# A decoder block's schedule: convolution steps metered by what VectorE already holds, small work moved between engines, a second pair of buffers for the second half's x

## The chip, the core and the metric

The kernel runs on one core of a Trainium2 chip. Its engines work side by side, each through its own list of instructions in order: TensorE (PE in the profile) multiplies matrices into PSUM, VectorE (DVE) and ScalarE (ACT) do elementwise work, GpSimd (POOL) elementwise work on SBUF, and SyncE (SP) issues most transfers. The metric is the device time of one execution in microseconds (us), as a median over runs.

## The reference

One layer of a decoder block over 2048 tokens of width 1024, in float32:

```python
h = rms_norm(x, norm_w) * (1 + scale) + shift            # scale, shift, gate = silu(c) @ w_ada + b_ada
a, b, g_conv, q, k, v, g_attn, m_conv, m_attn = split(h @ w_in)
u = a * sigmoid(b);  u = depthwise_causal_conv(u, 31 taps) + bias
u = silu(layer_norm(u)) * silu(g_conv);  y_conv = u @ w_conv_out
q, k = rope(rms_norm(q)), rope(rms_norm(k))              # 12 heads of 128
# three head groups, windows (128, 512, 2048) read with stride (1, 4, 16);
# their outputs are mixed by a softmax over the groups' log denominators
y_attn = (o * silu(g_attn)) @ w_attn_out
out = x + gate * ((sigmoid(m_conv) * y_conv + sigmoid(m_attn) * y_attn) @ w_out)
```

## The kernel before

**Products and slots.** Nearly all of PE's time goes to `h @ w_in`. Float32 operands are split into a high and a low part (`h`, `l`, names ending in _hi and _lo, and sh, sl for weights), and a product of two is three matmuls: high by high, low by high, high by low. A *quad* is a pair of 128-column blocks over half the tokens, computed with seven block products instead of eight; each product is twelve matmuls of 128x512 (L326) and is called a *slot*. There are 562 slots, in two halves of 1024 tokens: in each, first Q, K and V quads (half 0: slots 16 to 127; half 1: 282 to 407), then the quads of the gates, of the convolution's input (`ab_quad`) and of attention's gate (`ag_quad`), up to slots 281 and 561. Afterwards come the convolution branch's layer norm and the two branch projections (`ya`, `yc`, L1587), then the output projection (L1869).

**What goes on beside.** For each product ACT rounds the weights to the high part (L263) and POOL or DVE subtracts for the low part (L264; `lo_engines` names the products of a quad whose split goes to DVE). POOL also forms the weight differences of the seven-product scheme (L258). DVE adds the products' PSUM banks (L349, L364, L526).

Each of twelve *rotations* per half takes two heads of Q or K: ACT squares, DVE joins the squares (L609), PE sums them over the head (L618, pss), ACT adds the epsilon, PE turns the sums round (L629), POOL raises them to the power -1/2 (L638, `roots`), while DVE does the rotary products (L688 to L695). For K the factor must go back to rows: ACT `upper` (L650), DVE `lower` (L654), PE `turned_back` (L658, pwk), DVE `widen` (L662, rwk), PE `spread` (L667, rsk), DVE `key_scale` (L672). Group 2 is the one with stride 16; its rotations start a little later within their quad.

Each *ab quad* gives some 50 convolution steps to DVE (`conv_parts`): even taps and odd taps separately (L383 to L399), a join, and mixed taps on the sum of both (L415), which give the odd output tokens; POOL forms the sum. Attention runs in *units*, one begun every second slot: scores on PE, mask and minimum on DVE (L820), exponentials on ACT, transposes on PE (L836) copied by DVE into `pT` (L838), values on PE (L861), the mix of groups on DVE (L853, L864), a transpose back (L882). The second half's x is normalised beside the first half's slots 21 and later, four rounds of four tiles (`later_load`, `later_scale`, `later_sum`, lines 1319 to 1340), with one buffer a tile; attention starts when this is done, at slot 80.

**What sets the order.** The program walks through the slots and calls, at fixed places in each, what was booked with `at_slot(s, f, where)`: the places are, in order, enter, load, act, pe, vec, prepare, act2, then the product (with mid after its sixth matmul), tail and store. An engine's instructions stand in the order in which they were emitted, except in the gates of each half, where a scheduler orders DVE, ACT, POOL and SP; PE's list is always as emitted. Convolution steps are given out by count at the end of a slot:

```python
due += CONV_RATE                 # 3.1
if not conv_todo:
    due = 0.0
count = int(due)
due -= count
run_conv(count)
```

## Time and profile before

| | before |
|---|---|
| median of 3 runs | 2426.02 us (2423.64 to 2428.11) |
| profiled execution, its own time | 2425.99 us |
| span of the profile | 2423.9 us |
| PE, DVE, ACT, POOL busy | 2302.4, 1820.0, 1074.2, 1090.0 us |
| instructions | 34180 |

Busy time of an engine is the time in which at least one of its instructions runs. A row of the waits says which engine waited at which tile and line, for whose result, and then the total, the number of times and the longest in us. A timeline row has the start, the duration, the engine, the line and operation, and in brackets the idle time before it with what ended it. A row of windows has the window, its length, then PE, PEld (weight loads), DVE, ACT and POOL busy with the number of instructions, the clock granted to PE as a share, the busy share of the transfer engines and the GB/s moved.

### The profile page before, as it was taken

The page shows a single profiled execution, that of the slowest core. Times are in us where ns is not written, and L with a number is a line of the kernel's source. Part 1 is how long each engine was busy: PE and PEld are TensorE (multiplying, and loading weights), DVE is VectorE, ACT ScalarE, POOL GpSimd, SP SyncE. Part 2 cuts the span into 40 slices and gives each one's busy share as a digit, 9 for nine tenths or more (in the row PEclk, how much of TensorE's full clock was granted, in tenths as well). Part 3 has the DMA queues.
Part 4 walks back from the last instruction along what each step waited for, and adds up shares of the span by engine and source line. Part 5 has one row for each costly group of instructions (what it writes and reads, how often), then busy time and mean ns, then how long its engine had stood idle before and what let it go on. Part 6 is the DMA issues. An engine that isn't in the chain of part 4 may idle for free.

```text
span 2423.9 us, 34180 instructions
## 1 busy us (share of the span) xinstructions
PE 2302.4 (95%) x11242; PEld 1874.7 (77%) x11242; DVE 1820.0 (75%) x2976; ACT 1074.2 (44%) x2187; POOL 1090.0 (45%) x844
## 2 busy tenths in 40 slices
PE   6998889999989999899999999999999999999999
PEld 4776668778777888787778887887888877888887
DVE  6788786563999999937766557459999987787644
ACT  4753345445553444554445444553444444332221
POOL 2466454456445779855423333345556640000221
PEclk9998999999999999999999999999999999999999
DMA  7655655667554445643556665755444469876553
GB/s 254 197 175 187 200 182 168 195 187 244 177 178 141 166 165 187 230 153 107 169 173 182 200 185 161 251 170 187 142 132 154 141 211 333 291 237 192 179 160 105
DMA packets 304104, 451.50 MB, mean 186 GB/s; under 512 B 29236, under 2 KB 132788, under 8 KB 303928
## 3 DMA queue, kind: packets, MB, share of 16 engines
q1 hardware_dynamic: 289656, 423.62, 55.1%
q10 hardware_dynamic: 14272, 25.72, 2.9%
q8 instruction: 88, 1.44, 0.2%
q14 instruction: 88, 0.72, 0.1%
HBM read 284.98 MB, written 164.24 MB: 185 GB/s over the span
## 4 chain that ended last, share of the span: by engine, by line
PE 61%; DVE 9%; DMA 3%; issue 2%; POOL 1%; ACT 1%; SPq 0%; DVEq 0%; POOLq 0%; ACTq 0%
PE yc L1587 7%; PE paab L326 6%; PE oa L1869 4%; PE pag_ma_d L326 3%; PE pcab L326 3%; PE ya L1587 3%; PE pav L326 2%; PE paq L326 2%; PE pag_mc_d L326 2%; PE pak L326 2%; PE pag_g_d L326 2%; PE po L861 2%; PE oc L1869 2%; PE pbab L326 1%; PE pcg_ma_d L326 1%
## 5 line engine op out<-in xcount | busy, mean ns | idle before, releaser
L264 POOL TENSOR_TENSOR slT<-wT,shT 128x512 fp32r<-128x512 f32 x188 | 257.8, 1372 | 317.5 <-ACT shT L263 305.3
L264 POOL TENSOR_TENSOR slB<-wB,shB 128x512 fp32r<-128x512 f32 x142 | 188.3, 1327 | 169.2 <-ACT shB L263 153.9
L264 POOL TENSOR_TENSOR slT<-wB,shT 128x512 fp32r<-128x512 f32 x98 | 135.0, 1381 | 207.9 <-ACT shT L263 184.6
L263 ACT ACTIVATE shB<-wB 128x512 fp32r<-128x512 f32 x234 | 147.3, 630 | 182.8 <-issue 42.4
L263 ACT ACTIVATE shT<-wT 128x512 fp32r<-128x512 f32 x192 | 120.2, 627 | 147.2 <-issue 22.8
L386 DVE SCALAR_TENSOR_TENSOR ce<-ut,chan,ce 128x512 f32<-128x512 f32 x240 | 179.9, 750 | 3.4
L415 DVE SCALAR_TENSOR_TENSOR ce<-us,pair_taps,ce 128x512 f32<-128x512 f32 x240 | 180.0, 750 | 3.3 <-DVE ce L410 0.5
L820 DVE CUSTOM_DVE_ANT_0 sm<-ps,mask,rqq 128x256 f32<-128x256 f32 (+1 forms) x192 | 78.0, 443 | 103.8 <-PE ps L805 37.8
L399 DVE SCALAR_TENSOR_TENSOR cq<-ut,chan,cq 128x512 f32<-128x512 f32 x208 | 155.2, 746 | 0.0
L258 POOL TENSOR_TENSOR wB<-wB,wB 128x512 f32<-128x512 f32 x80 | 114.0, 1425 | 69.0 <-DVE slB L264 59.1
L263 ACT ACTIVATE shT<-wB 128x512 fp32r<-128x512 f32 x120 | 75.4, 628 | 97.8 <-PE paab L326 24.4
L838 DVE COPY pT<-ptp 128x512 f32<-128x512 f32 (+2 forms) x96 | 58.8, 612 | 45.4 <-PE ptp L836 44.9
L264 DVE TENSOR_TENSOR slB<-wB,shB 128x512 fp32r<-128x512 f32 x92 | 77.9, 847 | 14.0 <-ACT shB L263 12.4
L137 POOL TENSOR_SCALAR stf<-stf 128x4 f32<-128x4 f32 x4 | 1.9, 472 | 190.9 <-DVE stf L1625 144.1
L861 PE MATMUL po<-v,pT 128*128 128x128 f32 x560 | 81.7, 276 | 2.5 <-DVE pT L838 2.3
L861 PEld LDWEIGHTS po<-v,pT 128*128 128x128 f32 x560 | 75.3, 191 | 9.6 <-ACT spare_lo L341 1.8
L1797 ACT ACTIVATE yh<-yq 128x512 fp32r<-128x512 f32 x48 | 27.3, 623 | 118.9 <-POOL yq L1791 46.1
L827 ACT ACTIVATE sm<-sm,osb 128x256 f32<-128x256 f32 (+1 forms) x128 | 58.5, 460 | 12.9 <-issue 5.5
L836 PE MATMUL ptp<-ident,sm 128*128 128x128 f32 x332 | 52.7, 275 | 5.3 <-DVE stm L820 4.1
L258 POOL TENSOR_TENSOR wB<-wB,wT 128x512 f32<-128x512 f32 x40 | 57.6, 1439 | 0.0
L258 POOL TENSOR_TENSOR wT<-wB,wB 128x512 f32<-128x512 f32 x40 | 56.1, 1403 | 2.1
L836 PEld LDWEIGHTS ptp<-ident,sm 128*128 128x128 f32 x332 | 41.2, 140 | 20.1 <-issue 6.6
(833 smaller groups left out, 7803.1 us busy)
## 6 DMA issues: line engine op xcount, KB each, us to landing
wB<-in_w_in_dram SPq DMA_DIRECT2D x274, 256.0 KB, 4.2
wT<-tT_d SPq DMA_DIRECT2D x152, 256.0 KB, 2.9
tT_d<-wB SPq DMA_DIRECT2D x114, 256.0 KB, 3.5
qk<-qk_d SPq DMA_DIRECT2D x96, 256.0 KB, 4.5
v_d<-vev SPq DMA_DIRECT2D x48, 256.0 KB, 3.5
qk_d<-spare_hi SPq DMA_DIRECT2D x48, 256.0 KB, 3.9
qk_d<-spare_lo SPq DMA_DIRECT2D x48, 256.0 KB, 4.1
v<-v_d SPq DMA_DIRECT2D x96, 128.0 KB, 3.7
```

The source lines that it names most:

```text
L258: nc.gpsimd.tensor_tensor(dst, x0, x1, op=ALU.subtract)
L263: nc.scalar.activation(h, q[name], AF.Copy)
L264: eng.tensor_tensor(l, q[name], h.bitcast(F32), op=ALU.subtract)
L326: nc.tensor.matmul(ps, x, y, start=(first and m == 0), stop=(last and m == 11), skip_group_check=True)
L386: stt(box["e"], e[:, 1 + j : 513 + j], chan[:, cb, 2 * j : 2 * j + 1], box["e"], op0=ALU.mult, op1=ALU.add)
L399: stt(box["o"], o[:, 2 + j : 514 + j], w, psum_o, op0=ALU.mult, op1=ALU.add)
L415: stt(dst, box["both"][:, 1 + j : 513 + j], pair_taps[:, cb, j : j + 1], box["e"], op0=ALU.mult, op1=ALU.subtract if j == 0 else ALU.add)
L820: nc.vector.tensor_tensor_reduce(sm[:, a:z], ps[:, a:z], m[:, 256 - (z - a) :], rq[:, b, u % 2 : u % 2 + 1], 3e38, ALU.add, ALU.min, box[" ...
L836: nc.tensor.transpose(pt[:, c : c + P], box["sm"][:, c : c + P], ident)
L861: nc.tensor.matmul(po[:, P * i : P * i + P], box["pT"][:, c : c + P], vt, start=(m == 0), stop=(m == count[i] - 1))
L1587: nc.tensor.matmul(pz, w, xx, start=(m == 0), stop=(m == len(terms) - 1))
L1869: nc.tensor.matmul(ps, y, w, start=(m == 0 and ps.name not in begun), stop=(m == 11 and not more), skip_group_check=True)
```

## The change

1. Convolution steps are metered: a wrapper `vec` around VectorE adds 0.12 + size/860 (times 1.3 for a two-tensor operation on the size) for each DVE operation that goes through it, `spent`; at a slot's end the credit rises by 2.95 and falls by what was spent, and steps are run while it is above 0.35. Quads are ordered a little differently, so the first ab quad comes at slots 135 to 141 in half 0 (was 142 to 148) and 415 to 421 in half 1 (was 429 to 435); the last steps of half 0 may run until slot 294 (`AGAIN`).
2. The first even and odd tap of each ab quad, and half 0's copies `pT`, are done by ACT.
3. In half 0 the squares are not joined: PE sums both, accumulating.
4. `turned` becomes two transposes of 128x128. `lower` goes to POOL. For the groups other than 2 the K steps from `turned_back` on are booked half a slot sooner.
5. In half 0's gate, ab and ag quads the split of product 5 goes to POOL.
6. The second half's x has two buffers a tile; rounds 0 and 1 load at once, and attention starts at slot 71.
7. The rotary table's angle steps stand elsewhere: three ahead of the first modulation vector, none at the end of slot 0.

```diff
-FIRST_GATES, BETWEEN = (2, 3), ((1, 1, 1, 1, 2, 1, 2, 3), (1, 1, 2, 1, 1, 1, 1, 3))
-CONV_RATE = 3.1
+FIRST_GATES, BETWEEN = (1, 1), ((1, 2, 1, 2, 1, 2, 1, 3), (1, 1, 2, 1, 1, 2, 1, 4))
+PACE, AGAIN = (2.95, 2.95), 12
...
+            def call(out, *args, **kw):
+                size = 1
+                for d in out.shape[1:]:
+                    size *= d
+                spent[0] += 0.12 + size / 860 * (1.3 if name == "tensor_tensor" else 1.0)
+                return f(out, *args, **kw)
...
                 if j == 0:
                     box["e"] = bank("t", f"ce{half}_{cb}")
-                    nc.vector.tensor_scalar(box["e"], e[:, 1:513], chan[:, cb, 0:1], chan[:, cb, TAPS : TAPS + 1],
-                                            op0=ALU.mult, op1=ALU.add)
+                    nc.scalar.activation(box["e"], e[:, 1:513], AF.Identity, scale=chan[:, cb, 0:1], bias=chan[:, cb, TAPS : TAPS + 1])
...
-        return [*[even(j) for j in range(HT + 1)], add, *[odd(j) for j in range(HT)], join,
+        return [odd(0), *[even(j) for j in range(HT + 1)], add, *[odd(j) for j in range(1, HT)], join,
                 *[mixed(j) for j in range(HT + 1)], done]
...
+        def opened_ut():
+            while len(conv_todo) > 50:
+                run_conv(1)
...
-        def sums(c):
+        turns = []
+
+        def sums(c, i):
             def f():
-                if c == 0:
+                if not turns:
                     box["pr"] = bank("u", f"pss{n}")
-                pr, sq = box["pr"], box.pop(("sq", c, late[c]))
+                pr, sq = box["pr"], box.pop(("sq", c, i))
+                first, done = half or not turns, half or c in turns
+                turns.append(c)
                 for q in range(4):
                     nc.tensor.matmul(pr[32 * q : 32 * q + 32, P * c : P * c + P], sel, sq[:, P * q : P * q + P],
-                                     start=True, stop=True, skip_group_check=True)
+                                     start=bool(first), stop=bool(done), skip_group_check=True)
...
-                nc.tensor.matmul(pt[:, 8 * c : 8 * c + 8], box["rows"][:, c], ident.rearrange("p (q r) -> p q r", r=32)[:, :, :2],
-                                 start=True, stop=True)
+                nc.tensor.transpose(pt[:, P * c : P * c + P], box["rows"][:, c], ident)
...
-            tt(lo, r, hi.bitcast(F32), op=ALU.subtract)
+            nc.gpsimd.tensor_tensor(lo, r, hi.bitcast(F32), op=ALU.subtract)
...
-                (4, "tail"), (5, "vec"), (5, "tail"), (6, "act2"), (6, "tail"), (7, "vec"))
+                (4, "tail"), (4, "tail"), (5, "mid"), (5, "tail"), (6, "mid"), (6, "tail"))
...
-            nc.vector.tensor_copy(valid(pT), valid(pt))
+            if half:
+                vec.tensor_copy(valid(pT), valid(pt))
+            else:
+                nc.scalar.activation(valid(pT), valid(pt), AF.Copy)
...
-            return column_steps(half, A0 + P * cb, B0 + P * cb, () if half else (0, 5))
+            return column_steps(half, A0 + P * cb, B0 + P * cb, () if half else (0,))
...
-    at_slot(0, lambda: angle_steps(2), "tail")
-    at_slot(1, lambda: angle_steps(4))
-    at_slot(2, lambda: angle_steps(4))
-    at_slot(3, lambda: angle_steps(2))
+    for s, count in ((1, 3), (2, 4), (3, 2)):
+        at_slot(s, lambda count=count: angle_steps(count))
...
-            q = xh[name] = xh["p"].tile([P, 512], F32, tag=f"x{name}", name=f"xl{name}{k}", bufs=1)
+            q = xh[name, k] = xh["p"].tile([P, 512], F32, tag=f"x{name}", name=f"xl{name}{k}", bufs=2)
...
-        at_slot(when, lambda k=k: later_load(k), "store")
-        room = [r for r in room if r >= when + 2]
+        at_slot(LATER_0 + 1 if k < 2 else free[k - 2], lambda k=k: later_load(k), "store")
+        room = [r for r in room if r >= max(when, LATER_0 + 4)]
...
-        due += CONV_RATE
-        if not conv_todo:
-            due = 0.0
-        count = int(due)
-        due -= count
-        run_conv(count)
+        credit = min(max(credit, -2.0) + PACE[i >= half_jobs] - spent[0], 2.0)
+        spent[0] = 0.0
+        while conv_todo and credit > 0.35:
+            run_conv(1)
+            credit -= spent[0]
+            spent[0] = 0.0
```

In the rows below, the number in a tile's name that follows stk, pwk, rwk or pcv is the number of the rotation or quad, and 0, 1 and so on behind sm the group and block of an attention unit. Every operation that goes through the wrapper has line L208 after the change.

POOL around rotation 3 of K in half 0, before: only pow (L638) of the chain is here, between weight differences and splits.

```order
L258 TENSOR_TENSOR wB_0_3072_2846<-wB_0_3072_2850,wB_0_3072_2846 128x512
L258 TENSOR_TENSOR wT_0_3072_2922<-wB_0_3072_2852,wB_0_3072_2846 128x512
L638 TENSOR_TENSOR stk_3_2972<-stk_3_2972,mhalf 128x16
L264 TENSOR_TENSOR slT_0_3072_3044<-wT_0_3072_2922,shT_0_3072_3043 128x512
L258 TENSOR_TENSOR wB_0_3072_2850<-wB_0_3072_2852,wB_0_3072_2850 128x512
```

After the change `lower` (L680) stands right behind pow (L664), with nothing between them.

```order
L274 TENSOR_TENSOR wB_0_3072_2955<-wB_0_3072_2959,wB_0_3072_2955 128x512
L274 TENSOR_TENSOR wT_0_3072_3065<-wB_0_3072_2961,wB_0_3072_2955 128x512
L664 TENSOR_TENSOR stk_3_3118<-stk_3_3118,mhalf 128x16
L680 TENSOR_TENSOR stk_3_3118<-stk_3_3118 128x2x8
L280 TENSOR_TENSOR slT_0_3072_3211<-wT_0_3072_3065,shT_0_3072_3210 128x512
```

The same rotation on DVE, before: `lower` (L654) behind the rotary products and a split, then `widen` (L662).

```order
L693 SCALAR_TENSOR_TENSOR spare_hi<-spare_hi,hw,cos_1037 128x512
L694 TENSOR_TENSOR spare_hi<-spare_hi 128x512
L695 TENSOR_TENSOR spare_hi<-tmk_3_10_2979,tmk_3_11_2981 128x512
L264 TENSOR_TENSOR slB_0_3072_3014<-wB_0_3072_2848,shB_0_3072_3013 128x512
L654 TENSOR_TENSOR stk_3_2972<-stk_3_2972 128x2x8
L662 TENSOR_TENSOR rwk_3_3049<-pwk_3_3041,edge 32x512
L526 TENSOR_TENSOR spare_lo<-spare_lo,pcv_3_2956 128x32x16
```

After the change `lower` is gone from here, and `widen` (rwk) stands where it stood, behind the same products.

```order
L208 ISA osb_0_1_3166 128x1
L208 SCALAR_TENSOR_TENSOR spare_hi<-spare_hi,hw,cos_1037 128x512
L208 TENSOR_TENSOR spare_hi<-spare_hi 128x512
L208 TENSOR_TENSOR spare_hi<-tmk_3_10_3134,tmk_3_11_3136 128x512
L208 TENSOR_TENSOR slB_0_3072_3174<-wB_0_3072_2957,shB_0_3072_3173 128x512
L208 TENSOR_TENSOR rwk_3_3216<-pwk_3_3208,edge 32x512
L208 TENSOR_TENSOR spare_lo<-spare_lo,pcv_3_3102 128x32x16
```

VectorE beside an attention unit in half 0's gates, before: convolution steps (ce, cq), the mask (sm), pT's copy and a sum of products.

```order
L386 SCALAR_TENSOR_TENSOR ce_0_5494<-ut_0_5265,chan,ce_0_5494 128x512
L399 SCALAR_TENSOR_TENSOR cq_0_5726<-ut_0_5265,chan,cq_0_5726 128x512
L830 TENSOR_REDUCE stm_0_2_5540<-stm_0_2_5540 128x2
L349 TENSOR_TENSOR spare_lo<-spare_lo,pbg_mc_d_4_5550 128x512
L838 COPY pT_0_0_5570<-ptp_0_0_5566 128x384
L386 SCALAR_TENSOR_TENSOR ce_0_5494<-ut_0_5265,chan,ce_0_5494 128x512
L264 TENSOR_TENSOR slB_0_8704_5605<-wB_0_8704_5326,shB_0_8704_5604 128x512
L399 SCALAR_TENSOR_TENSOR cq_0_5726<-ut_0_5265,chan,cq_0_5726 128x512
L843 TENSOR_TENSOR stm_0_2_5540<-stm_0_2_5540 128x6
L386 SCALAR_TENSOR_TENSOR ce_0_5494<-ut_0_5265,chan,ce_0_5494 128x512
L864 SCALAR_TENSOR_TENSOR osb_0_0_5462<-po_0_0_5621,stm_0_0_5463,part_0_0_5389 128x128 x2
L399 SCALAR_TENSOR_TENSOR cq_0_5726<-ut_0_5265,chan,cq_0_5726 128x512
```

After the change, at an attention unit of the same stage: the copy of pT is gone from this engine, and one to four steps stand between two operations of the unit.

```order
L208 SCALAR_TENSOR_TENSOR ce_0_5472<-ut_0_5414,chan,ce_0_5472 128x512
L208 SCALAR_TENSOR_TENSOR cq_0_5470<-ut_0_5414,chan,cq_0_5470 128x512
L208 SCALAR_TENSOR_TENSOR ce_0_5472<-ut_0_5414,chan,ce_0_5472 128x512
L208 SCALAR_TENSOR_TENSOR cq_0_5470<-ut_0_5414,chan,cq_0_5470 128x512
L208 TENSOR_TENSOR stm_0_4_5484<-stm_0_4_5484 128x6
L208 SCALAR_TENSOR_TENSOR ce_0_5472<-ut_0_5414,chan,ce_0_5472 128x512
L208 SCALAR_TENSOR_TENSOR cq_0_5470<-ut_0_5414,chan,cq_0_5470 128x512
L208 TENSOR_REDUCE stm_0_4_5484<-stm_0_4_5484 128x2
L208 TENSOR_TENSOR spare_hi<-spare_hi,pbg_mc_d_2_5546 128x512
L208 SCALAR_TENSOR_TENSOR ce_0_5472<-ut_0_5414,chan,ce_0_5472 128x512
L208 SCALAR_TENSOR_TENSOR osb_0_2_5391<-po_0_2_5562,stm_0_2_5392,part_0_2_5315 128x128 x2
L208 SCALAR_TENSOR_TENSOR cq_0_5470<-ut_0_5414,chan,cq_0_5470 128x512
```

VectorE at the start of the first branch projection, before: yt are the gated sums of ya, red and d belong to the first block of the layer norm, which stands ahead of them.

```order
L415 SCALAR_TENSOR_TENSOR ca_7_18560<-us_7_18424,pair_taps,ce_7_18303 128x512
L426 TENSOR_TENSOR usum<-usum,ca_7_18560 128x1024
L1613 SCALAR_TENSOR_TENSOR d_18706<-pm_18789,d_18706 128x512 x6
L1617 TENSOR_TENSOR red_18791<-red_18791,sq_1_18795 128x512
L1613 SCALAR_TENSOR_TENSOR d_18706<-pm_18789,d_18706 128x512 x2
...
L1617 TENSOR_TENSOR red_18791<-red_18791,sq_7_18819 128x512
L1701 SCALAR_TENSOR_TENSOR yt_0_18723<-ma_0_18697,ya_0_18699 128x512
L1137 TENSOR_TENSOR ai_0l<-fraw,ai_0h 128x512
L1701 SCALAR_TENSOR_TENSOR yt_1_18747<-ma_1_18726,ya_1_18728 128x512
```

After the change yt_0 and yt_1 stand ahead of that block, which now starts behind yt_2 and is cut by yt_3.

```order
L208 TENSOR_TENSOR spare_lo<-spare_lo,pcg_g_d_6_18626 128x512
L1732 SCALAR_TENSOR_TENSOR yt_0_18795<-ma_0_18769,ya_0_18771 128x512
L1732 SCALAR_TENSOR_TENSOR yt_1_18819<-ma_1_18798,ya_1_18800 128x512
L208 TENSOR_TENSOR ai_0l<-fraw,ai_0h 128x512
L208 TENSOR_TENSOR ai_1l<-fraw,ai_1h 128x512
L208 TENSOR_TENSOR wc0l_18829<-fraw,wc0h_18828 128x512
L1732 SCALAR_TENSOR_TENSOR yt_2_18849<-ma_2_18822,ya_2_18824 128x512
L1644 SCALAR_TENSOR_TENSOR d_18778<-pm_18861,d_18778 128x512 x6
L1732 SCALAR_TENSOR_TENSOR yt_3_18906<-ma_3_18852,ya_3_18854 128x512
L1648 TENSOR_TENSOR red_18863<-red_18863,sq_1_18867 128x512
L1644 SCALAR_TENSOR_TENSOR d_18778<-pm_18861,d_18778 128x512 x2
```

130 lines of the change are left out of this document (72 added, 58 removed).

## The prediction

> **What bounds the kernel now.** I read the page first (engine shares and the chain that ended last), then the waits of PE, then busy time by stage, then single stalls on the timeline.
>
> ```profile
> span 2423.9 us, 34180 instructions
> PE 2302.4 (95%) x11242; PEld 1874.7 (77%) x11242; DVE 1820.0 (75%) x2976; ACT 1074.2 (44%) x2187; POOL 1090.0 (45%) x844
> PE 61%; DVE 9%; DMA 3%; issue 2%; POOL 1%; ACT 1%; SPq 0%; DVEq 0%; POOLq 0%; ACTq 0%
> ```
>
> PE is the bound: 2423.9 - 2302.4 = 121.5 us without a matmul, and the chain leaves PE mostly for DVE. So nearly all that this change can win is those 121.5 us, and the slow matmuls that follow a stall. Who ends the stalls:
>
> ```profile
> PE pwk L658 <- DVE stk L654: 23.2, 11, 5.6
> PE pssk L618 <- DVE sqk L609: 7.6, 7, 2.2
> PE pssq L618 <- DVE sqq L609: 7.5, 3, 4.7
> PE rsk L667 <- DVE rwk L662: 6.5, 6, 1.9
> PE ya L1587 <- DVE yt L1701: 5.5, 2, 5.0
> PE pav L326 <- ACT spare_hi L465: 5.3, 1, 5.3
> PE pta L882 <- DVE osb L864: 5.1, 5, 2.0
> PE ptp L836 <- DVE stm L820: 4.1, 3, 1.6
> PE pag_ma_d L326 <- ACT spare_hi L341: 4.0, 1, 4.0
> ```
>
> The columns are total, times, longest. The nine rows hold 68.8 us, and the change touches the place of each. By stage (PE, PEld, DVE, ACT, POOL busy, then the granted clock): two pieces of the first half's Q/K/V, its gates beside attention, its gates after attention, the second half's Q/K/V.
>
> ```profile
> 165.30:294.40 129.10, 109.50 (x501) 84.15 (x502) 113.00 (x134) 47.43 (x82) 71.42 (x44) 0.91 0.56 181
> 294.40:529.50 235.10, 218.80 (x1155) 178.09 (x1153) 161.22 (x275) 108.34 (x255) 112.31 (x73) 0.98 0.60 186
> 600.00:754.00 154.00, 140.45 (x738) 116.90 (x738) 152.75 (x371) 79.52 (x219) 76.01 (x76) 0.99 0.55 175
> 754.00:1017.00 263.00, 261.92 (x1154) 216.05 (x1153) 253.89 (x360) 122.95 (x215) 206.94 (x162) 1.00 0.52 178
> 1088.00:1528.00 440.00, 422.07 (x2352) 350.11 (x2351) 279.28 (x504) 206.94 (x474) 170.32 (x123) 0.98 0.58 173
> ```
>
> In the first piece PE misses 19.6 us and DVE is the denser engine (113.0); between 600 and 754 DVE is full (152.75 of 154) while PE misses 13.5. From 754 on PE misses only 1.1 although DVE is still 97% busy: no gain is left there. In the second half DVE is 63% busy and PE still misses 17.9, so those stalls are short chains that come late, not lack of DVE.
>
> **The change part by part.** The sum is made against the profiled execution, 2426.0 us, which is the median of the runs (2426.02).
>
> *K chains.* One rotation of K ends in pow on POOL, `upper` on ACT, `lower` on DVE (now POOL), pwk on PE, rwk on DVE, rsk on PE.
>
> ```profile
> 268.79 0.39 PE L326 MATMUL paq<-A_hi,shB 128*128 128x512 f32 x1
> 271.28 0.39 PE L326 MATMUL paq<-A_hi,slB 128*128 128x512 f32 x1
> 277.27 0.37 PE L658 MATMUL pwk<-ident,stk 128*32 128x128 f32 x1 [5.59 <-DVE stk L654]
> 282.69 0.81 PE L667 MATMUL rsk<-rwk,pick 32*128 32x512 f32 x2
> 278.37 0.67 DVE L662 TENSOR_TENSOR rwk<-pwk,edge 32x512 fp32r<-32x512 f32 x1
> 346.60 3.38 POOL L638 TENSOR_TENSOR stk<-stk,mhalf 128x16 f32<-128x16 f32 x1
> 355.41 1.23 DVE L654 TENSOR_TENSOR stk<-stk 128x16 fp32r<-128x16 f32 x1
> 356.79 0.37 PE L658 MATMUL pwk<-ident,stk 128*32 128x128 f32 x1 [5.36 <-DVE stk L654]
> 357.19 0.68 DVE L662 TENSOR_TENSOR rwk<-pwk,edge 32x512 fp32r<-32x512 f32 x1 [0.55 <-PE pwk L658]
> ```
>
> The first two rows are the first and last of a product's 12 matmuls: 2.49 us for 11 steps, 2.72 for a whole one, a slot. Behind the 5.59 us gap the next product, 277.27 to 282.69, took 5.4: the gap costs another 2.7. At 356.79 pow had ended at 350.0, and `lower` started at 355.41 behind DVE's rotations. Right behind pow on POOL it could end near 351. But rwk stays on DVE, in the same queue: at 357 it could start about 355.5, so rsk comes near 356.3 where it came near 361.9 (gap plus slow product). Won there: about 5. At 277, DVE's queue holds rwk until about 278.3 whatever `lower` does: pwk moves to 271, the wait goes to rsk at about 279 rather than 282.7, less slow matmuls after the new gap: about 2. Together -7, bounds 0 (rwk takes the whole stall) and -15 (both stalls and their slow products go). In the second half 9.5 us of the pwk row lie between 1088 and 1528 with DVE idle a third of the time; with the same slow-clock share (half a gap) 14, of which I take 9, as the waits now come half a slot (1.36) sooner for the groups without a late turn: bounds 0 and -14.
>
> *The squares' sums.* 24 joins leave DVE, PE adds 24 sets of eight small matmuls.
>
> ```profile
> L609 DVE TENSOR_TENSOR sqq<-sqq,sqq 128x512 f32<-128x512 f32 x24 | 20.1, 837 | 15.4 <-ACT sqq L603 15.3
> 148.87 0.43 PE L618 MATMUL pssk<-sqk,sel 128*32 128x128 f32 x8 [1.12 <-DVE sqk L609]
> 264.13 0.61 PE L629 MATMUL prqk<-ident,ssrk 128*128 128x8 f32 x4
> ```
>
> A join is 0.84 (mean of Q's in both halves): 24 are 20 us of DVE at most. The sets cost PE 24 x 0.35 to 0.43 = +8.4 to +10.3. Two transposes for the four small matmuls of `turned` (0.61) can at most save half of that, 24 x 0.3 = 7; I take 4. PE's own work: +4.5, bounds +2 and +10. Of the two pss rows 13 us are the first half's, 10.6 of it in the DVE-bound piece. Later x, with a second pair of buffers, puts work of 0.75 an operation into that same piece: with each row of the two orders of instructions at its mean, 101.5 us of DVE work where 104 stood, so waits there turn up at the next DVE result. I count 3 of the 10.6, the 2.4 outside, and 4 for slow matmuls and a wait on a bank at 329: -9, bounds 0 and -18.
>
> *Convolution beside attention.*
>
> ```profile
> 748.30 0.74 DVE L399 SCALAR_TENSOR_TENSOR cq<-ut,chan,cq 128x512 f32<-128x512 f32 x1
> 748.96 0.67 DVE L364 TENSOR_TENSOR spare_lo<-spare_lo,pcg_ma_d 128x512 f32<-128x512 f32 x1
> 749.55 0.34 DVE L864 SCALAR_TENSOR_TENSOR osb<-po,stm,part 128x128 f32<-128x128 f32 x1
> L838 DVE COPY pT<-ptp 128x512 f32<-128x512 f32 (+2 forms) x96 | 58.8, 612 | 45.4 <-PE ptp L836 44.9
> ```
>
> Attention's osb stands behind a convolution step, and PE's transpose waits for it. Steps start 0.66 apart (748.30 to 748.96), and the new rule books 0.12 + 512/860 = 0.715 for one; so 2.95 booked are 2.72 us, exactly a slot without attention. Between 600 and 754 a slot lasts about 4.2 us (37 slots), so DVE gets 65% of the time instead of 99%, pT's copies (0.61 each) and the first taps leave it, and attention begins nine slots sooner. ACT takes both: 79.5 of 154 is busy, and some 16 copies and 6 taps are 13 us more if each takes what it took on DVE. Waits of 13.5 and some 3 of slow matmuls: I take -12, bounds -4 (waits for ACT's copies in DVE's place) and -17. In the slots after attention the pace fills DVE exactly, as before; no gain, and the debit rule keeps a backlog from growing.
>
> *Splits on POOL.*
>
> ```profile
> L264 DVE TENSOR_TENSOR slB<-wB,shB 128x512 fp32r<-128x512 f32 x27 | 26.4, 979 | 2.2 <-ACT shB L263 1.9
> L415 DVE SCALAR_TENSOR_TENSOR ce<-us,pair_taps,ce 128x512 f32<-128x512 f32 x80 | 60.1, 751 | 1.0
> L264 POOL TENSOR_TENSOR slB<-wB,shB 128x512 fp32r<-128x512 f32 x13 | 16.8, 1295 | 2.1 <-ACT shB L263 2.1
> ```
>
> These are groups between 754 and 1017. Some 14 of the 22 moved splits lie there: 14 x 1.295 = 18 us on POOL, 206.9 to 225 of 263 (86%). Most hide; the quads that also load attention's gate come closest to full: +2, bounds 0 and +13 (eight such quads late by one split and its slow matmuls). The Trainium skill speaks against the move: its GPSIMD Engine Reference (4.1 Engine selection) puts two-input elementwise work on VectorE, GpSimd being about twice as slow, and 8 (Key points) names contention with DVE instructions that have two SBUF inputs. The first holds in direction only, 1.295 against 0.979; by a factor of two the 14 would cost 27 us, and POOL would stand at 234. The second fits the splits' 979; the convolution step, one of whose inputs is in PSUM, keeps 751 beside it.
>
> *Start.*
>
> ```profile
> 27.23 0.17 DVE L973 TENSOR_TENSOR mod<-pt_ada,cols 128x8 f32<-128x8 f32 x1 [2.86 <-PE pt_ada L970]
> 42.03 1.23 DVE L1012 SCALAR_TENSOR_TENSOR spare_hi<-spare_hi 128x1024 f32<-128x1024 f32 x1
> 43.51 0.33 PE L940 MATMUL xm<-ident,xrow 128*128 128x128 f32 x1 [3.25 <-DVE xrow L936]
> ```
>
> The angle steps no longer stand ahead of xrow: 3.25 and 2 of slow matmuls go. Three now fill the 2.86 us hole ahead of L973, 3 x 1.23 = 3.7, or twice that beside POOL: +1 to +4. I take -3, bounds -5 and +2.
>
> *Changes of stage.* At 1028 PE waits 5.3 (pav) behind convolution steps on DVE; the steps now stand behind the S_lo block, but 27 of them run on into the second half and hold a PSUM bank until slot 294: 0, bounds -8 and +5. The pag_ma_d wait (4.0, 6 with slow matmuls) loses its convolution steps since the second half's convolution starts 14 slots sooner: -4, bounds -6 and +3.
>
> ```profile
> 1993.54 4.66 DVE L1617 TENSOR_TENSOR red<-red,sq 128x512 f32<-128x512 f32 x6
> ```
>
> This block of the first norm stood ahead of yt, which PE waited 5.0 for; yt 0 and 1 now stand ahead of it. Gap and slow matmuls are 7: -6, bounds -7 and +1.
>
> The sum: -7 - 9 (K) + 4.5 - 9 (squares) - 12 - 4 - 6 - 3 + 2 + 0 = -43.5, so 2382.
>
> **Rivals.** *DVE stays the bound in Q/K/V.* Each wait removed there returns at rwk or at a PSUM eviction: K and squares give nothing, 25 lost, 2407. For it: 113.0 of 129.1, and later x in the same piece. Against: DVE is 69% busy after 294 and 63% in the second half.
>
> *Pace or POOL disappoint.* Attention's waits pass to ACT's pT copies (12 lost), or POOL is late in eight quads (11 lost): 2394 either way.
>
> *Everything comes off:* all terms at their good ends but PE's own work: 2382 - 8 - 5 - 9 - 5 - 2 - 1 - 2 = 2350.
>
> *Slower: K's shorter deadlines.* Eight rotations of K (the groups without a late turn, both halves) must now have pwk and rsk ready half a slot sooner. If `lower`, waiting on POOL for ACT's `upper`, holds up POOL's splits, or is held by them, each pays 2 x 1.36 plus 2.7 of slow product, 8 x 5.4 = 43, and both K terms are lost, 16: 2441. It decides once `lower` ends over 1.4 us after the middle of that product. For it: pow alone takes 3.38, and in the second half little of the chain is DVE's. Against: nothing stands between pow and `lower` on POOL, and pow ended 1.4 us ahead of the wait at 356.79's gap.
>
> **How the numbers follow.** Forecast 0.46, of its own 2362 to 2402; DVE-bound 0.20; pace or POOL 0.14; everything 0.12; slower 0.08. The range 2352 to 2414 leaves out the slower case, half of the best one and little else. A measurement of this kernel tells about 0.2% (5 us) from no change. Faster: the first four less the tails, 0.87; same 0.05; slower 0.08.
>
> **What would show it.** Right: pwk waits under 8 us in all, pss under 5, rsk grown to 8 to 15; DVE under 80% between 600 and 754 with PE idle under 4; no yt wait over 1; no xrow wait. Wrong: slT or pwk of POOL among the first waits, PE idle still near 20 in the 129 us piece, PE idle in the slots after attention, where there was none.

## The result

The changed kernel takes 2384.7 us (median; 2382.15 to 2389.96) against 2424.83 us of the kernel before on the same chip: a ratio of 0.9835, 95% interval 0.9816 to 0.9855, so 1.65% faster. The profiled execution has a span of 2382.7 us, 41.2 less than before. The forecast was 2382 with a range of 2352 to 2414. The total came out; several of the terms that made it did not, and two had the wrong cause. Medians below are over all executions of a kernel; one of the six of the meter alone took 8051.8 us and is left out of its ratio.

The page of the changed kernel, its first lines (xN is the number of instructions):

```profile
span 2382.7 us, 34400 instructions
PE 2293.4 (96%) x11386; PEld 1864.2 (78%) x11386; DVE 1740.3 (73%) x2838; ACT 1113.5 (47%) x2267; POOL 1120.5 (47%) x878
```

PE now misses 89.3 us instead of 121.5. Its busy time also fell by 9 although 144 instructions were added; part of this is that fewer matmuls stand slow behind a stall (165 of the products' took over 0.55 us, 191 before). DVE lost 80 us of work, ACT and POOL took 39 and 31. Ten of PE's waits after the change (tile waited at, whose result, us, times, longest):

```profile
PE pcv L342 <- DVE spare_hi L208: 7.3, 2, 4.4
PE pssk L644 <- ACT sqk L625: 4.8, 2, 2.9
PE pwk L684 <- POOL stk L680: 4.8, 3, 2.2
PE pag_ma_d L342 <- ACT spare_lo L357: 2.0, 2, 1.0
PE pag_mc_d L342 <- ACT spare_hi L357: 2.3, 2, 2.1
PE rsk L693 <- DVE rwk L208: 2.0, 2, 1.7
PE pssq L644 <- DVE sqq L208: 1.9, 1, 1.9
PE pssq L644 <- DVE spare_lo L208: 1.8, 2, 1.0
PE pav L342 <- ACT spare_hi L487: 1.3, 1, 1.3
PE xm L972 <- DVE xrow L968: 1.1, 2, 0.6
```

pwk, 23.2 before, is 4.8 and waits for POOL; the wait of ya for yt is gone from the list; rsk fell from 6.5 to 2.0 where it was forecast to grow. A new entry stands high: pcv, 7.3; of all waits only xm's at the start is longer (9.9, 9.1 before). The windows of the stages shown of before: slots 36 to 68, 68 to 128 and 148 to 184 as there, then 184 to 281 (there to 280) and the second half's Q/K/V, slots 296 to 407 (there 302 to 411):

```profile
164.20:288.80 124.60, 109.11 (x557) 82.78 (x556) 107.83 (x133) 48.68 (x83) 72.16 (x46) 0.95 0.66 215
288.80:512.60 223.80, 222.25 (x1289) 180.89 (x1287) 136.01 (x255) 120.44 (x305) 108.03 (x76) 1.00 0.64 191
590.10:720.70 130.60, 126.34 (x652) 106.19 (x651) 113.04 (x272) 76.70 (x192) 75.41 (x71) 1.00 0.59 193
720.70:988.50 267.80, 265.76 (x1166) 219.52 (x1165) 236.09 (x315) 131.08 (x226) 227.24 (x179) 0.99 0.51 177
1042.00:1470.00 428.00, 417.52 (x2315) 344.89 (x2314) 268.03 (x461) 208.86 (x466) 176.61 (x128) 0.99 0.59 179
```

Slots 68 to 128 lost nearly all their idle time (16.3 to 1.5); slots 36 to 68 kept most of theirs (19.6 to 15.5), DVE still the dense engine there. Slots 184 to 281 took 2.1 us longer than before.

A third view is worked out from the products' starts: the time at which a slot begins, less the same time in the kernel before. Between two columns stands what a stretch gave. All are profiled executions, and one can stand some us from its kernel's median: the cap's 5.7 below it, counting's 5.3 and the split's 4.4 above.

| slot | 16 | 128 | 184 | 281 | 310 | 407 | 561 | end |
|---|---|---|---|---|---|---|---|---|
| the change | -0.8 | -16.9 | -33.8 | -31.7 | -24.7 | -34.0 | -32.3 | -41.2 |
| steps by count | -1.4 | -14.4 | -27.4 | -25.9 | -26.5 | -37.5 | -35.4 | -44.3 |
| ACT's work back on DVE | -2.3 | -16.8 | -27.1 | -29.0 | -6.4 | -15.4 | -15.1 | -23.5 |
| split 5 back on DVE | -1.2 | -13.0 | -22.5 | -23.3 | -13.0 | -23.1 | -19.7 | -28.6 |
| K chain at its old places | -1.6 | -13.7 | -27.2 | -29.0 | -26.4 | -36.3 | -34.0 | -43.0 |
| one buffer for x | -2.7 | -14.3 | -24.5 | -22.8 | -18.2 | -29.2 | -29.6 | -38.0 |
| credit capped at 3.0 | -1.0 | -16.2 | -33.6 | -35.5 | -36.0 | -46.6 | -45.8 | -54.3 |
| before, with meter only | +0.3 | +2.3 | +1.8 | +1.6 | +14.5 | +13.3 | +9.5 | +10.2 |
| before, with ACT's work only | -0.4 | -0.8 | -1.4 | -2.5 | -4.2 | -4.7 | -6.2 | -15.0 |

The change, counting, the split and the cap differ in nothing up to slot 128 but stand at -13.0 to -16.9 there: differences of up to 4 us in a stretch of one execution say nothing. In the change attention begins at slot 71 and not at 80, so 316 of its matmuls (tiles ps, ptp, po and pta) stand ahead of slot 128 where 266 stood. From start to start they take 35.5 us there, 31.0 before, so 4.5 us moved from the stretch 128 to 184 into the one before: net of this the Q/K/V stretch gave 20.6 (16 to 20 in the three kernels like it), the stretch beside attention 12.4.

The changed kernel just behind slot 282, DVE and PE:

```profile
1022.42 1.27 DVE L208 TENSOR_TENSOR slB<-wB,shB 128x512 fp32r<-128x512 f32 x1
1023.62 1.01 DVE L208 TENSOR_TENSOR spare_hi<-spare_hi,pcv 128x512 f32<-128x512 f32 x1
1024.55 1.53 DVE L208 SCALAR_TENSOR_TENSOR ce<-us,pair_taps,ce 128x512 f32<-128x512 f32 x2
1024.68 0.80 PE L342 MATMUL pcv<-S_hi,shB 128*128 128x512 f32 x1 [4.40 <-DVE spare_hi L208]
1025.27 0.63 PE L342 MATMUL pcv<-S_lo,shB 128*128 128x512 f32 x1
```

A V quad's eviction (1023.62) stands behind convolution steps of the first half and a split, and PE waits 4.4 us for its bank; the rows of 0.63 behind it are half-rate matmuls. The stretch with this wait is the one in which the table shows 7 us going back, 281 to 310.

### The profile page after: what moved, and what is told of

It reads as the page before. It is cut to its first block, busy times and chain, and to the rows that moved or that the text cites. A ratio compares the mean times of both kernels' runs of the same rounds, so it can differ in the third digit from the quotient of the medians.

```text
span 2382.7 us, 34400 instructions
## 1 busy us (share of the span) xinstructions
PE 2293.4 (96%) x11386; PEld 1864.2 (78%) x11386; DVE 1740.3 (73%) x2838; ACT 1113.5 (47%) x2267; POOL 1120.5 (47%) x878
## 5 line engine op out<-in xcount | busy, mean ns | idle before, releaser
L280 POOL TENSOR_TENSOR slB<-wB,shB 128x512 fp32r<-128x512 f32 x164 | 219.1, 1337 | 187.8 <-ACT shB L279 176.7
L208 DVE SCALAR_TENSOR_TENSOR ce<-us,pair_taps,ce 128x512 f32<-128x512 f32 x240 | 180.8, 753 | 5.9
L208 DVE SCALAR_TENSOR_TENSOR ce<-ut,chan,ce 128x512 f32<-128x512 f32 x240 | 180.4, 751 | 0.8
L208 DVE SCALAR_TENSOR_TENSOR cq<-ut,chan,cq 128x512 f32<-128x512 f32 x208 | 156.3, 751 | 4.5 <-ACT cq L409 4.3
L208 DVE CUSTOM_DVE_ANT_0 sm<-ps,mask,rqq 128x256 f32<-128x256 f32 (+1 forms) x192 | 78.1, 444 | 95.1 <-PE ps L837 36.0
L1828 ACT ACTIVATE yh<-yq 128x512 fp32r<-128x512 f32 x48 | 27.4, 624 | 119.8 <-POOL yq L1822 46.2
L208 DVE TENSOR_TENSOR slB<-wB,shB 128x512 fp32r<-128x512 f32 x70 | 55.4, 791 | 30.6 <-ACT shB L279 24.4
L1887 DVE TENSOR_TENSOR xt<-xt,oa 128x512 f32<-128x512 f32 x32 | 22.0, 687 | 45.8 <-PE oa L1900 45.8
```

Source lines behind the costliest of these rows:

```text
L208: return f(out, *args, **kw)
L280: eng.tensor_tensor(l, q[name], h.bitcast(F32), op=ALU.subtract)
L1828: nc.scalar.activation(h, src, AF.Copy)
L1887: add = lambda dst, ps: tc.keep_in_program_order(nc.vector.tensor_tensor(dst, dst, ps, op=ALU.add))
```

## The experiments

Each kernel is the changed one with the edit shown, or the one before where that is said. Medians are set against the change's 2384.7; ratios, with their 95% intervals in brackets, are to the kernel before on the same chip, whose medians beside these runs lie between 2424.8 and 2426.9. Where an interval overlaps the change's (0.9816 to 0.9855), the difference is not certain: the squares, the old places, the cap, the split, `lower`, one buffer, and the first kernel of the last pair.

**Steps by count again.**

```diff
-        credit = min(max(credit, -2.0) + PACE[i >= half_jobs] - spent[0], 2.0)
-        spent[0] = 0.0
-        while conv_todo and credit > 0.35:
-            run_conv(1)
-            credit -= spent[0]
-            spent[0] = 0.0
+        credit += 3.1
+        if not conv_todo:
+            credit = 0.0
+        count = int(credit)
+        credit -= count
+        run_conv(count)
```

> The changed kernel, with convolution steps given out by count again (3.1 a slot) and all the rest kept, ACT's taps and copies and the quads' order among it. Theory 1 (the meter carries the stage beside attention): attention's small operations stand behind up to four steps again; PE's idle time in the first half's gates beside attention (slots 140 to 184) goes from about 7 us back to 15 or more, and the time rises by 8 to 15 us, to 2393 to 2400. Theory 2 (what left DVE carries it: 48 copies and 16 taps less, some 40 us): the time stays within 4 us of 2385.

2376.11 us (0.9792, 0.9776 to 0.9808): 8.6 us faster than with the meter. Theory 1 is refuted, and theory 2 does not say it either. The table places it: nothing that can be told from scatter is lost beside attention, and the 7 us between slots 281 and 310 are not lost, since counting leaves no step at slot 282. The pav wait of the kernel before is there again, 5.5.

**ACT's work back on DVE.**

```diff
-                    nc.scalar.activation(box["e"], e[:, 1:513], AF.Identity, scale=chan[:, cb, 0:1], bias=chan[:, cb, TAPS : TAPS + 1])
+                    vec.tensor_scalar(box["e"], e[:, 1:513], chan[:, cb, 0:1], chan[:, cb, TAPS : TAPS + 1], op0=ALU.mult, op1=ALU.add)
...
-                    nc.scalar.activation(box["o"], o[:, 2:514], AF.Copy, scale=w)
+                    vec.tensor_scalar(box["o"], o[:, 2:514], w, None, op0=ALU.mult)
...
-            if half:
-                vec.tensor_copy(valid(pT), valid(pt))
-            else:
-                nc.scalar.activation(valid(pT), valid(pt), AF.Copy)
+            vec.tensor_copy(valid(pT), valid(pt))
```

> The changed kernel, with the first taps and the first half's copies of pT on DVE again, metering kept. Theory 1 (the meter carries it): the copies and taps are booked, so fewer steps run beside attention and the convolution ends some slots later; the stage beside attention keeps its gain and the time rises by no more than 5 us (2385 to 2390). Theory 2 (the work moved off DVE carries it): 40 us of DVE work come back, the convolution has 30 to 50 steps more left over at the second half's start, and the time rises by 8 to 20 us (2393 to 2405).

2403.42 us (0.9907, 0.9893 to 0.9922), 18.7 slower: theory 2's number. But most of the loss has one place, PE's first wait in that kernel:

```profile
PE ptv L606 <- DVE ca L208: 19.5, 1, 19.5
```

50 steps are left at slot 282 (27 in the change) as the program counts them, and the traces show 45 (25) taps on DVE behind it; at slot 294 the rest is run in one piece, and V's transposes wait 19.5 us for the PSUM bank that the last steps hold. Between 128 and 184 it loses 6.6 us, a little above scatter.

**Squares joined on DVE again.**

```diff
-            if half == 0:
-                at_slot(max(s, e6), sums(c, i), "tail")
...
-            if half:
-                at_slot(joins[c][0], joined(c), joins[c][1])
-                at_slot(added[c][0], sums(c, late[c]), added[c][1])
+            at_slot(joins[c][0], joined(c), joins[c][1])
+            at_slot(added[c][0], sums(c, late[c]), added[c][1])
```

> The changed kernel, with the first half's squares joined on DVE again and summed by PE once, at their old places. By the prediction's terms PE wins back 8.4 us (24 sets of eight at 0.35) and DVE's 24 joins cost waits of about 9 us: 2382 to 2390, PE waits for pss up from 8.5 to about 15 us. Rival (DVE is no bound in this stage any more): waits stay, PE's 8.4 us come off, 2376 to 2379.

2377.87 us (0.9801, 0.9782 to 0.9819); its profiled span, 2380.4, is 2.3 below the change's. Waits for pss, in this kernel:

```profile
PE pssq L644 <- DVE sqq L208: 6.6, 5, 3.1
PE pssk L644 <- DVE sqk L208: 5.2, 5, 1.8
```

11.8 us where the change has 8.5 by all releasers: DVE's waits are back in part, PE's extra sets are gone, and slot 128 begins at -18.2, inside the scatter of -16.9. From start to start PE's sums of the first half took 14.7 us in the change and 9.1 here, a price of 5.6 where 8.4 was forecast. The exchange of joins for sums on PE gave nothing that these runs can tell, or lost a little.

**The K chain at its old places.**

```diff
-                (4, "tail"), (4, "tail"), (5, "mid"), (5, "tail"), (6, "mid"), (6, "tail"))
+                (4, "tail"), (5, "vec"), (5, "tail"), (6, "act2"), (6, "tail"), (7, "vec"))
```

> The changed kernel, with the K chain's last steps booked where they were before for the groups other than 2 (lower still on POOL). If the half slot taken from the chain costs (the pwk waits for POOL's lower, 4.8 us with as much in slow matmuls), the time falls by 3 to 8 us, 2377 to 2382, and pwk leaves the list of waits. If the earlier place costs nothing, or frees the squares' and K's buffers sooner, the time stays within 2 us or rises by up to 5 us.

2386.05 us (0.9839, 0.9818 to 0.9859): the same. The waits changed places:

```profile
PE rsk L693 <- DVE rwk L208: 14.1, 8, 3.5
PE pwk L684 <- POOL stk L680: 2.1, 3, 0.9
```

With the old places PE waits 14.1 for rwk and 2.1 for `lower`; with the new ones 2.0 and 4.8. So the forecast's "the wait goes to rsk" holds for the move of `lower` alone, and the half slot is what removed it. In the table the old places lose 4.0 between slots 16 and 128 and 3.4 from there to 184, and win 4.4 between 281 and 310, where pcv is 4.5 and not 7.3; each is near the scatter, so why 9 us less of these waits bring nothing in the total stays open.

**A cap of 3.0 on the credit.**

```diff
-        credit = min(max(credit, -2.0) + PACE[i >= half_jobs] - spent[0], 2.0)
+        credit = min(max(credit, -2.0) + PACE[i >= half_jobs] - spent[0], 3.0)
```

> The changed kernel, with the credit capped at 3.0 and not at 2.0, so that four steps fit into a slot in which DVE holds nothing else (with 2.0 it is three, whatever the pace); no step is then left at the second half's first slot, where the change leaves 27. Theory 1 (those leftovers cause the 4.4 us wait at the second V quad and the waits for PSUM banks behind it): the 7 us that the change loses between slots 281 and 310 come back, 2376 to 2379, the level of counting. Theory 2 (four steps a slot overfill DVE): PE begins to wait in the gates between slots 184 and 281, where it waited for about 2 us, and the time stays at 2383 to 2392.

2377.07 us (0.9799, 0.9772 to 0.9825), theory 1's number, and that of counting, which leaves no step either. From 281 to 310 it gains 0.5 where the change loses 7.0, and nothing is lost between 184 and 281. The pcv wait is gone; the old pav wait of the kernel before is back:

```profile
PE pav L342 <- ACT spare_hi L487: 5.4, 1, 5.4
```

**The meter alone, on the kernel before** (the wrapper, the credit, the late opening of ut and the leftover until slot 294; no other part of the change).

```diff
-CONV_RATE = 3.1
+PACE, AGAIN = (2.95, 2.95), 12
...
-        due += CONV_RATE
...
+        credit = min(max(credit, -2.0) + PACE[i >= half_jobs] - spent[0], 2.0)
```

> The kernel before, with the metering alone: steps by what DVE holds, the convolution's input tile opened late, the leftover allowed until slot 294; the order of quads, all engines and all other places as before. It leaves 42 steps at slot 282 (the change leaves 27) and 40 at the end. Theory 1 (metering by itself only shifts steps out of the stage beside attention and into the two ends): 5 to 10 us are won beside attention, 15 to 25 are lost where the second half's V quads wait for a PSUM bank and some at the end: 2430 to 2445, slower than before. Rival (metering is the gain, as the change's first line reads): 2405 to 2418.

2438.89 us, ratio 1.0049 (1.0032 to 1.0066): slower than before. The window of slots 148 to 184:

```profile
602.00:756.00 154.00, 141.25 (x744) 117.67 (x743) 152.71 (x371) 80.16 (x219) 76.24 (x77) 0.99 0.55 176
```

Two of its waits:

```profile
PE ptv L608 <- DVE ca L208: 13.8, 1, 13.8
PE ya L1611 <- DVE yt L208: 5.8, 2, 5.1
```

Not even theory 1's 5 to 10 us beside attention are there: DVE is as full as before (152.7 of 154) and PE as idle (12.8, was 13.5). In this stage the scheduler orders DVE, and the meter only says at which slot a step is handed to it. What the meter does change is how many steps are left at slot 282: 42 (none before), and there it costs 13.8 us at ptv. The 40 expected at the end cost nothing: the trace has 8 taps on DVE behind the start of slot 561, as before, and from there to the end the kernel loses 0.7.

**ACT's work alone, on the kernel before** (first taps and half 0's pT on ACT, the odd first tap ahead of the even ones as in the change, count kept).

```diff
-                    nc.vector.tensor_scalar(box["o"], o[:, 2:514], w, None, op0=ALU.mult)
+                    nc.scalar.activation(box["o"], o[:, 2:514], AF.Copy, scale=w)
...
-            nc.vector.tensor_copy(valid(pT), valid(pt))
+            if half:
+                nc.vector.tensor_copy(valid(pT), valid(pt))
+            else:
+                nc.scalar.activation(valid(pT), valid(pt), AF.Copy)
```

> The kernel before, with only the first taps and the first half's copies of pT moved to ACT; steps by count, all else as before. If what left DVE carries the stage beside attention, PE's 13.5 us idle between slots 148 and 184 falls to about 6 and the time to 2412 to 2418. If the stage needs the earlier start of attention and of the convolution too, it falls to 10 or 11 and the time stays at 2420 to 2425.

2410.07 us (0.9933, 0.991 to 0.9956): the number of the first theory, the place of neither.

```profile
599.00:753.00 154.00, 144.33 (x756) 120.01 (x755) 148.97 (x361) 91.38 (x245) 79.86 (x79) 0.99 0.57 181
```

A wait that this kernel has and the one before has not:

```profile
PE po L863 <- ACT pT L840: 3.6, 2, 2.8
```

PE's idle time from 148 to 184 falls by 4 only, and PE now waits for ACT's pT; DVE stays 97% full, with steps enough waiting to fill what was freed. The table shows 8.8 of the 15 us of this execution behind slot 561: ya no longer waits for yt.

**Product 5's split back on DVE.**

```diff
-            return column_steps(half, A0 + P * cb, B0 + P * cb, () if half else (0,))
+            return column_steps(half, A0 + P * cb, B0 + P * cb, () if half else (0, 5))
...
-        return column_steps(half, c0, c0 + P, () if half else (0,))
+        return column_steps(half, c0, c0 + P, () if half else (0, 5))
```

> The changed kernel, with product 5's split of the first half's gate, ab and ag quads on DVE again (22 splits, 0.61 apart when nothing disturbs, booked as 0.89). By the prediction's term of +2 for POOL the time would fall to about 2383. If what DVE holds decides when the convolution ends, 20 booked units are 27 steps more left at the second half's start (54), and the time rises by 10 to 25 us, to 2395 to 2410, all of it behind slot 281.

2392.75 us (0.9859, 0.983 to 0.9888), 8 slower than the change, a little under the expected range. That the splits belong on POOL is likely and not certain, as the intervals overlap. The place was not the expected one: of the 12.5 us of the profiled execution 7 are beside attention and 3 behind slot 281, where the trace shows 31 taps (25 in the change) and the bank wait is back:

```profile
PE ptv L606 <- DVE ca L208: 6.4, 1, 6.4
```

**`lower` back on DVE.**

```diff
-            nc.gpsimd.tensor_tensor(lo, r, hi.bitcast(F32), op=ALU.subtract)
+            tt(lo, r, hi.bitcast(F32), op=ALU.subtract)
```

> The changed kernel, with K's lower half subtracted on DVE again, at the change's places. By the prediction's K terms (7 in the first half, 9 in the second, of which lower's place is most) PE's pwk waits rise from 4.8 us to 15 or more with as much in slow matmuls, and the time by 8 to 18 us, 2393 to 2403. Rival (the waits went because DVE is less loaded and rwk decides anyway): pwk stays under 9 us and the time within 4 us of 2385.

2390.99 us (0.9871, 0.9842 to 0.99), 6 slower, between the two. The waits are near what the forecast's K terms have:

```profile
PE pwk L684 <- DVE stk L208: 16.9, 8, 7.1
```

16.9 for 4.8, though not the 23.2 of before: the stall of 5.36 at 356.79 comes back with 1.6 only. The longest is the stall that was 5.59 at 277, a rotation of group 2, whose places did not move.

**One buffer for the second half's x.**

```diff
-            q = xh[name, k] = xh["p"].tile([P, 512], F32, tag=f"x{name}", name=f"xl{name}{k}", bufs=2)
+            q = xh[name, k] = xh["p"].tile([P, 512], F32, tag=f"x{name}", name=f"xl{name}{k}", bufs=1)
...
-        at_slot(LATER_0 + 1 if k < 2 else free[k - 2], lambda k=k: later_load(k), "store")
-        room = [r for r in room if r >= max(when, LATER_0 + 4)]
+        at_slot(when, lambda k=k: later_load(k), "store")
+        room = [r for r in room if r >= when + 2]
```

> The changed kernel, with one buffer a tile for the second half's x, loaded and spread as before, so attention starts some nine slots later and more of its units run beside the convolution. Theory 1 (the early attention is worth more than the crowding of DVE before slot 68 costs): slots 36 to 68 win 1 to 4 us, the stage beside attention loses them again, and more convolution steps are left at slot 282 (over 40): the time rises by 8 to 20 us, 2393 to 2405. Rival (the second buffers only move the same work): within 4 us of 2385.

2384.17 us (0.9831, 0.9808 to 0.9855): the rival. Attention's earlier start is worth nothing in the total: slot 184 begins at -24.5 instead of -33.8, but most stretches behind it do a little better than in the change (from 281 to 310 4.6 are lost instead of 7.0), and the end is at -38.0. The steps over 40 expected at slot 282 did not come; the trace has 27 taps there (25). Two waits of the first half are in this kernel that the change has not, a bank's and a longest rsk of 4.2:

```profile
PE pck L342 <- DVE spare_hi L208: 3.8, 1, 3.8
PE rsk L693 <- DVE rwk L208: 5.4, 3, 4.2
```

The first is the wait on a bank at 329 that the forecast put to the squares: the three other kernels with one buffer have it too, and none with two.

**Three small edits together: cap 3.0, the first half's pace 3.3, two angle steps ahead of the first modulation vector; and the same with the joins on DVE.**

```diff
-PACE, AGAIN = (2.95, 2.95), 12
+PACE, AGAIN = (3.3, 2.95), 12
...
-    angle_steps(3)
+    angle_steps(2)
...
-    for s, count in ((1, 3), (2, 4), (3, 2)):
+    for s, count in ((1, 4), (2, 4), (3, 2)):
```

> The changed kernel with three small edits: the credit capped at 3.0, the first half's pace 3.3 a slot, and two angle steps ahead of the first modulation vector in place of three. The convolution of the first half is then given out by slot 271, ahead of the block of input splits at slots 275 to 281. If the 5.4 us wait at the second half's first V quad that was left with the cap alone comes from steps among these splits, it goes, and with 1 us at the start the time is 2366 to 2373 (the cap alone: 2377). If it comes from the splits themselves, the time stays at 2374 to 2379.

> The kernel with cap 3.0, pace 3.3 and two angle steps ahead, and the first half's squares joined on DVE as before the change. If the joins are worth the 7 us that the single run of them showed (2378 against 2385), this is 4 to 8 us faster than the same kernel without the joins; if PE's 8.4 us and DVE's waits cancel, as the waits and the slots' starts say, the two agree within 3 us.

2375.59 us (0.9797, 0.9771 to 0.9823) and, with the joins, 2370.5 us (0.9782, 0.9762 to 0.9802). The start gained: slot 16 begins at -3.4 and -3.3, where the nine kernels with three angle steps there begin between -0.8 and -2.7. The pav wait stayed, 5.3, and the order on DVE ahead of it shows that handing the steps out earlier did not move them:

```profile
981.87 3.12 DVE L208 SCALAR_TENSOR_TENSOR ce<-us,pair_taps,ce 128x512 f32<-128x512 f32 x4
984.89 2.96 DVE L208 TENSOR_TENSOR S_lo<-landingS,S_hi 128x512 fp32r<-128x512 f32 x2
987.77 0.74 DVE L208 SCALAR_TENSOR_TENSOR ce<-us,pair_taps,ce 128x512 f32<-128x512 f32 x1
988.43 1.09 DVE L208 TENSOR_TENSOR S_lo<-landingS,S_hi 128x512 fp32r<-128x512 f32 x1
989.45 0.67 DVE L208 TENSOR_TENSOR spare_hi<-spare_hi,pcg_g_d 128x512 f32<-128x512 f32 x1
```

All steps had been given out by slot 271, but the scheduler that orders this stage still sets them between the splits of the next half's input, and the last sum (989.45), whose result frees pav's bank by way of ACT, stands behind both. Whether steps or splits cost the 5.3 us is therefore not told. The joins' 5 us are not certain, as the two intervals overlap; with the earlier pair (7 us, overlapping too) they point the same way, that the sums on PE are no gain. This last kernel is the fastest that was run, 14 us below the change, 2.2% below the kernel before.

## Why the prediction was right, and where it was not

*The total* (2382 for 2384.7) is a sum in which errors met, so that it came so near is in part luck: the first half's Q/K/V gave about twice its share, the start gave less, and the changes of stage took where a gain was forecast. Of the signs named, pwk (4.8), yt and xrow (0.6 at most) came; pss is 8.5 (under 5 was forecast), rsk 2.0 (8 to 15), DVE 87% between slots 148 and 184 (under 80) with PE idle 4.3 (under 4). Of the signs of being wrong, pwk waiting for POOL is among the first waits. The best case of 2350 leaves out two good ends that the forecast names, 8 at the pav wait and 2 of the splits; with them it is 2340.

*K and squares, first half: -7 and -9, with +8.4 and about -2 of PE's own work, so some -10; measured 20.6.* Ahead of slot 68, in the DVE-bound piece, the forecast held (slots 36 to 68 gained 4.5, idle 19.6 to 15.5, the stall at 277 came back as pcv 2.9 at 269 and rsk 1.7 at 276). The step that failed is the one behind it: there the forecast kept rsk waits, and PE misses 1.5 of 223.8 us. Also, the second pair of x buffers had no gain in the sum, only work put into the crowded piece. With one buffer, where attention stands as before, slots 16 to 128 give 11.6, near the forecast, and the pck and rsk waits are there; so it is likely that the surplus came with the second pair. The total did not keep it. "rsk grown to 8 to 15" was wrong, since the half slot that the rival priced as a danger removed those waits (14.1 with the old places). That rival, the shorter deadlines, met one row of its forecast, pwk <- POOL 4.8, and cost no more than this.

*The squares' exchange.* The term's two sides, PE's sums and DVE's waits, nearly cancel, as summed; joins on DVE are as fast or 5 us faster.

*K, second half: -9.* From slot 310 to 407 the change gained 9.3, from 296 to 407 5.7, part of it catching up behind the bank waits. pwk fell as forecast, and `lower` is shown to be the cause of most of it: back on DVE, pwk is 16.9.

*Convolution beside attention: -12, measured 12.4 in the change (8.5 with counting, 10.2 with one buffer), but not for the reason given.* That the size came out is luck. The forecast read the pace of 2.95 as a slot's worth of DVE time and took the meter for the cause. The cap of 2.0 on the credit comes first: in a slot in which DVE holds nothing else three steps fit, not four. DVE is at 87% from 148 to 184 (65% forecast) and, from 184 to 281, at 88% where it was 97%: the reserve is not used, and 27 steps are left. And the order in this stage is the scheduler's. The meter alone gives nothing; ACT's work alone little; taken out of the whole, ACT's part costs 7 us of the stretch and the split's 7, each little above the scatter of 4. So the gain beside attention seems to need DVE's load to fall by several of these at once; no run took them out together.

*Splits on POOL: +2, measured about -8, not certain.* The sign was most likely wrong, by the step that gave DVE's freed time no price because PE had no idle time after slot 184. It had one beside attention and at the second half's start. POOL did come to 227 of 268 us, 85% (86% forecast), without a stall in the list. The Trainium skill's GPSIMD Engine Reference (4.1 Engine selection), which would keep such two-input work on VectorE, holds in direction for the operation (1.337 on POOL against 0.791 on DVE, means of slB, 1.7 times) and probably not for this kernel, where the slower engine had the room.

*Changes of stage: 0 and -4, measured +7.0 (281 to 310) and +1.7 (407 to 561).* The leftover was named and its bank too, but bounded at +5, without a row that showed where V's evictions would stand among the steps; they stood behind them. That the cause is the leftover is shown by the cap and by counting, which leave none (+7.0 becomes -0.5 and -0.6), and, in the other direction, by 42 and 50 steps left (13.8 and 19.5 us at ptv). The pag_ma_d wait halved (4.0 to 2.0), and waits of 2.3 at pag_mc_d came in its place.

*Start: -3, measured -0.8 (down to -2.7 in kernels with the same start).* xrow's wait went (3.2 to 0.6 at most). The three steps cost what their upper part of the range said:

```profile
27.51 2.17 DVE L1044 SCALAR_TENSOR_TENSOR spare_hi<-spare_lo,spare_hi 128x1024 f32<-128x1024 f32 x1
29.60 0.15 DVE L1005 TENSOR_TENSOR mod<-pt_ada,cols 128x8 f32<-128x8 f32 x1
31.72 0.79 PE L342 MATMUL pC<-A_hi,shB_p 128*128 128x512 f32 x1 [3.38 <-ACT A_hi L1023]
```

The modulation vector starts at 29.60 and not at 27.23; two steps fit into the hole, the third, 2.17 long, does not.

*ya: -6, measured -8.9* (slot 561 to the end). The wait is gone. It is gone as well with ACT's work alone, and stays with the meter alone. The traces tell these apart. In the kernel before, and with the meter alone, 8 taps start on DVE behind the start of slot 561 (1976.0 before), the norm's block follows them, and the first yt stands behind it:

```profile
1982.43 0.75 DVE L415 SCALAR_TENSOR_TENSOR ca<-us,pair_taps,ce 128x512 f32<-128x512 f32 x1
1998.12 0.68 DVE L1701 SCALAR_TENSOR_TENSOR yt<-ma,ya 128x512 f32<-128x512 f32 x1
```

With ACT's work alone, and in every other kernel, no tap starts behind that slot's start (1969.8 here), and the first yt stands ahead of the block:

```profile
1967.08 0.73 DVE L414 SCALAR_TENSOR_TENSOR ca<-us,pair_taps,ce 128x512 f32<-128x512 f32 x1
1973.97 0.69 DVE L1703 SCALAR_TENSOR_TENSOR yt<-ma,ya 128x512 f32<-128x512 f32 x1 [3.82 <-DMA ma<-ma_d]
```

So the wait goes with a convolution that ends behind the last product. The forecast named the order of yt and the block and not what brings it about; that this is the cause was not tried by itself.

## What to carry to other kernels

A rule that meters filler work is worth no more than the place to which it pushes the work: look first at what is left over when the stage ends, and which buffers the leftover holds. Read a limiter by the clause that binds (here the cap, not the pace), and check whether the stage's order is the program's at all. When an engine is full, single offloads give little in that stage and may still pay at its end; when another engine is slower at an operation but has room, moving the work there may still pay. And look at what a part of a change does to the waits of other parts: here the second pair of buffers removed waits that the forecast had put to the squares.

## What the runs showed of the hardware that was not expected

Four executions with the same instructions up to slot 128 began that slot between 512.6 and 516.5 us; single stretches of profiled executions differ by up to 4 us with nothing changed, so stage ledgers below that size need the timed rounds beside them. Behind the 4.40 us gap at 1024.68 the product's matmuls start 0.43 us apart for about a product, where 0.23 is usual; behind the 1.86 us gap at 197.08 seven do so. But not every long gap has this behind it: after the 2.93 us gap at 250.15 in the same trace they start 0.23 apart at once, and after the 3.76 us gap at 329.10 in the kernel before too.
